# A column of norms that becomes rows through DRAM, in a two-block layer on one NeuronCore

## The chip, the cores and the metric

The kernel runs on one core of a Trainium2 chip. Its engines run side by side, each with its own queue, in order: TensorE (PE, with weight loads shown as PEld), VectorE (DVE), ScalarE (ACT), GpSimd (POOL) and SyncE (SP), which only starts DMA transfers. DMA transfers are also started from the queues of ACT and POOL. The metric is the device time of one execution in microseconds; lower is better.

## The reference

512 tokens of 1024 features pass through two blocks, in float32. The first has a mixing layer of 8 softmax-attention heads and 4 gated recurrent heads (HGRN), a cross-attention to 256 memory tokens, and a feed-forward layer. The second has a convolution branch, a state-space branch with 8 groups of 4 heads, and a gated feed-forward layer. What the change touches are two normalizations inside them. Each recurrent head of 128 features is normalized by the root of its mean square per token, before its gate:

```python
rec = hgrn2_chunkwise(gq, gf, gi, lbs[l])
rec = rmsnorm(rec, hgrn_norm_g[l]) * jax.nn.silu(gg...)   # per head of 128 features
h = h + jnp.concatenate([fox_out, rec], axis=-1) @ w_out[l]
...
def rmsnorm(x, g):
    y = x * lax.rsqrt(jnp.mean(x * x, axis=-1, keepdims=True) + EPS)
    return y * g
```

In the state-space branch each of the 8 groups of 256 features is gated and normalized in the same way, and a product with a 2048 x 1024 weight follows.

## The kernel before, in words

Tensors lie feature-major: a tile holds 128 features on the partitions and the 512 tokens along the free axis. A large product (`gemm_tile`) takes weights of 1024 x 128 at a time: SP's queue loads them, ACT casts them to a high part `wh` (L138), DVE computes the residual `wl` (L139), each into one of three buffers. For each of eight chunks PE makes three products 128x512, high by high (L150), the low part of one by the high of the other (L151, L152), which accumulate in a PSUM bank named `acc`. There are three `acc` banks, two each of `pa` and `pb`, and one `pc`. `gemm_tok` makes a token-major product and uses `pc` for its fourth tile.

A norm needs one number per token, on every partition. `col_sum` makes four products of a 128-token slice of squares with a column of ones (L223): the sums stand in a column, 128 tokens on the partitions and one column per slice. `rsqrt_col` scales them on DVE (L229) and raises them to −1/2 on POOL (L231). `row_bc` then makes four products in which the column, broadcast to 128 columns, is the stationary operand and the identity the moving one (L238); PSUM then holds the 512 values as a row on all 128 partitions. In float32 each of these is recorded as two matmuls.

Two users of this path matter here. `hgrn_out(i, AT)` writes one recurrent head, squares it, and multiplies it by the row in `pc` (L497). It is called for heads 0 and 1, and later for heads 2 and 3, in a stretch where PE also works on the attention's products and score transposes (L522), whose masks POOL adds (`fox_probs`). `group_b(g, ys, zs)` does the same for two tiles of a group (L942), and splits them into high and low parts (L201, L202). Its result is needed by `ssm_half(0)`, called in the fifth group for the first four, and `ssm_half(1)`, called after the eighth.

Next to these, `group_a` makes, per pair of heads of a group, a run of small products into `pb` (L916) whose operands come from ACT (L906) and DVE (L907), and reads rows of DRAM on all partitions by POOL's DMA (`ab`, L901; `ep`, L922). DVE also does the convolutions (L784, L807).

The order on each engine is made when the program is built: a scheduler takes the instructions in the order of the code, moved by `tc.high_priority(n)`. A negative n puts them later, so that other work already written fills in: `HPRI` is 80, `APRI` 60, `BPRI` 120. On the chip each engine keeps the order it was given.

Of the kernel before, what the change touches and what calls it, by code (L numbers as in the profile page):

```python
# [6 lines left out]
F32 = mybir.dt.float32  # L7
# [4 lines left out]
ALU = mybir.AluOpType  # L12
# [4 lines left out]
P = 128  # L17
S = 512
# [14 lines left out]
HPRI = 80  # L33
# [10 lines left out]
BPRI = 120  # L44
# [24 lines left out]
def _build(tc, nc, es, a, out):  # L69
    V, A, T, G = nc.vector, nc.scalar, nc.tensor, nc.gpsimd  # L70
# [8 lines left out]
    nrm = es.enter_context(pool("nrm", 2))  # L79
# [12 lines left out]
    def mC():  # L92
        return psc.tile([P, S], F32, tag="pc", name="pc")

    def ctile(shape, dt, name):
        return const.tile(shape, dt, tag=name, name=name)
# [3 lines left out]
    ones = ctile([P, P], F32, "ones")  # L100
    V.memset(ones, 1.0)
    es_mem, es_mx = es.enter_context(ExitStack()), ExitStack()
    mhalf = ctile([P, 4], F32, "mhalf")
    V.memset(mhalf, -0.5)

    pm = es_mem.enter_context(pool("pm", 1, side="right", reuse_waits="tile"))
# [4 lines left out]
    with tc.high_priority(3000):  # L111
        for k in range(0, 8, 2):
# [1 line left out]
            (nc.sync if k in (0, 6) else nc.gpsimd).dma_start(out=t, in_=memp[:, k:k + 2, :])  # L114
            mt += [t[:, 0, :], t[:, 1, :]]
            nc.sync.dma_start(out=raw0[:, k:k + 2, :], in_=a["w_xk"][0][:, k:k + 2, :])
    warm = nrm.tile([P, 4], F32, tag="rv", name="warm")
    A.copy(out=warm, in_=ones[:, 0:4])

    wps = psc.tile([P, S], F32, tag="pc", name="pc")  # L120
# [2 lines left out]
    ident = ctile([P, P], F32, "ident")  # L123
# [4 lines left out]
    def vcol(name, i=0, n=1):  # L128
        c, k = VEC[name]
        assert i + n <= k  # L130
        return vec[:, c + i:c + i + n]
# [76 lines left out]
    def sq_acc(accum, k, src, scale=1.0):  # L208
        if k == 0:
            A.activation(out=accum, in_=src, func=AF.Square, scale=scale)  # L210
        else:
            sq = nrm.tile([P, S], F32, tag="sq", name="sq")
            n = accum.shape[-1]
            A.activation(out=sq[:, :n], in_=src, func=AF.Square, scale=scale)
            V.tensor_tensor(out=accum, in0=accum, in1=sq[:, :n], op=ALU.add)

    def col_sum(accs, nt, ms=mA):

        ps = ms()
        accs = accs if isinstance(accs, list) else [accs]  # L220
        for j in range(nt):
            for i, ac in enumerate(accs):
                T.matmul(out=ps[:, j:j + 1], lhsT=ac[:, j * P:(j + 1) * P], rhs=ones[:, 0:1], start=i == 0,  # L223
                         stop=i == len(accs) - 1)
        return ps[:, :nt]

    def rsqrt_col(ps, nt, n, eps=EPS, name="r"):
        v = nrm.tile([P, 4], F32, tag="rv", name="rv")
        V.tensor_scalar(out=v[:, :nt], in0=ps, scalar1=1.0 / n, scalar2=eps, op0=ALU.mult, op1=ALU.add)  # L229
        r = nrm.tile([P, 4], F32, tag="rc", name="rc", bufs=4)  # L230
        G.tensor_tensor(out=r[:, :nt], in0=v[:, :nt], in1=mhalf[:, :nt], op=ALU.pow)  # L231
        return r[:, :nt]

    def row_bc(col, nt, ms=mA):

        ps = ms()
        for j in range(nt):
            T.matmul(out=ps[:, j * P:(j + 1) * P], lhsT=col[:, j:j + 1].to_broadcast([P, P]), rhs=ident, start=True,  # L238
                     stop=True)
        return ps[:, :nt * P]  # L240

    def norm(srcs, n, nt, gain=None, eps=EPS, pl=None, rtag="R", ms=mA, late=0):

# [75 lines left out]
    with ExitStack() as ea:  # L319
# [163 lines left out]
        def hgrn_out(i, AT):  # L483
            ps = mA()
            for j in range(4):
                T.matmul(out=ps[:, j * P:], lhsT=iT[:, j, i * P:(i + 1) * P],
                         rhs=AT[:, ab(j, j):ab(j, j) + 4 - j, :].rearrange("p a b -> p (a b)"),
                         start=j == 0, stop=j == 3)
            o_ = hslot(4 + i)
            mix[4 + i] = o_  # L490
            A.copy(out=o_, in_=ps)
            ac = nrm.tile([P, S], F32, tag="sqa", name="sqa")
            sq_acc(ac, 0, o_)
            with tc.high_priority(-HPRI):
                r = rsqrt_col(col_sum(ac, 4, mC), 4, P)
            with tc.high_priority(-2 * HPRI):
                V.scalar_tensor_tensor(out=o_, in0=o_, scalar=vcol("hgrn_norm_g"), in1=row_bc(r, 4, mC), op0=ALU.mult,  # L497
                                       op1=ALU.mult)

        def fox_probs(p, e, j, ps, nF, PT):  # L500

# [66 lines left out]
        hd = [hgrn_in(0), hgrn_in(1)]  # L568
        AT = hgrn_chain(hd)
        g_tok(iT, a["w_gi"])  # L570
        hgrn_out(0, AT[0])
        hgrn_out(1, AT[1])
        g_qk(0)
        g_qk(1)
        g_tok(vT, a["w_fv"])
        fox((0, 1))
        hd = [hgrn_in(2), hgrn_in(3)]
        AT = hgrn_chain(hd)
        hgrn_out(2, AT[0])
        hgrn_out(3, AT[1])  # L580
        g_qk(2)
        g_qk(3)
        fox((2, 3))
# [346 lines left out]
    def group_b(g, ys, zs):  # L930

        ac = nrm.tile([P, S], F32, tag="sqa", name="sqa")
        for e in range(2):
            V.tensor_tensor(out=zs[e], in0=ys[e], in1=zs[e], op=ALU.mult)
            sq_acc(ac, e, zs[e])
        with tc.high_priority(-APRI):
            r = rsqrt_col(col_sum(ac, 4, mC), 4, 256)
        with tc.high_priority(-BPRI):
            Rg = row_bc(r, 4, mC)
            res = []  # L940
            for e in range(2):
                V.scalar_tensor_tensor(out=zs[e], in0=zs[e], scalar=vcol("ssm_norm_g_2", 2 * g + e), in1=Rg, op0=ALU.mult,  # L942
                                       op1=ALU.mult)
                res.append(split_act(zs[e]))
        return res
# [294 lines left out]
```

## Time and profile before

| | |
|---|---|
| median of 3 runs | 1916.11 us (1915.81 to 1916.19) |
| profiled execution | 1916.54 us |
| its span | 1914.8 us |
| mean granted TensorE clock | 0.997 of full speed |
| DMA moved | 208.84 MB, mean 109 GB/s |

In the rows below, a line of a timeline has its start, its duration, the engine, the line of the program, the operation, the tiles (written <- read) with their shapes and count, and in square brackets the time the engine stood idle before it and what ended that. Matmuls are pipelined: the duration of one is longer than the distance to the next, and their ends are modelled, so distances between starts tell more than durations. A clock of 1.00 is the full level. "Waits" list who stood for whom, in total and how often.

### The profile page before, as it was taken

How to read it: one execution, taken by the hardware profiler on the slowest of the kernel's cores; microseconds unless marked ns; L12 is line 12 of the kernel's file. 1: busy time of each engine (PE TensorE's matmuls, PEld its weight loads, DVE VectorE, ACT ScalarE, POOL GpSimd, SP SyncE). 2: the span in 40 equal slices, each digit the busy share in tenths (PEclk: the TensorE clock that was granted, in tenths of full speed). 3: DMA queues.
4: the chain of work that ended last, by engine and by line, in shares of the span. 5: the costliest groups of instructions: out<-in, count | busy, mean ns of one | idle time of the engine just before them, and what ended most of it. 6: DMA issues, size and time to landing. Idle time of an engine off the chain costs nothing.

```text
span 1914.8 us, 25080 instructions
## 1 busy us (share of the span) xinstructions
PE 1892.4 (99%) x9680; PEld 1573.7 (82%) x9680; DVE 1207.1 (63%) x1886; ACT 861.7 (45%) x1393; POOL 101.8 (5%) x198
## 2 busy tenths in 40 slices
PE   9999999999999999999999999999999999999997
PEld 8887776877888888877888888888888988888897
DVE  6744756655443344467888989578997774324456
ACT  6524547444331233348545553545344653222344
POOL 1001110000000000011110110110000000000000
PEclk9999999999999999999999999999999999999999
DMA  7412212322323333344333333333345532233244
GB/s 259 132 57 86 67 54 80 100 66 78 94 95 98 99 99 104 110 95 142 119 122 108 108 119 105 107 115 103 102 141 186 165 91 98 83 116 98 90 130 145
DMA packets 67542, 208.84 MB, mean 109 GB/s; under 512 B 8536, under 2 KB 15448, under 8 KB 67424
## 3 DMA queue, kind: packets, MB, share of 16 engines
q1 hardware_dynamic: 57856, 184.09, 30.9%
q0 software_dynamic: 5968, 16.87, 3.0%
q10 hardware_dynamic: 3600, 6.30, 0.9%
q8 instruction: 76, 1.25, 0.3%
q14 instruction: 42, 0.34, 0.1%
HBM read 198.71 MB, written 8.54 MB: 108 GB/s over the span
## 4 chain that ended last, share of the span: by engine, by line
PE 51%; issue 2%; DVE 1%; DMA 1%; ACT 0%; POOL 0%; POOLq 0%; DVEq 0%; ACTq 0%
PE acc L150 16%; PE acc L151 16%; PE acc L152 16%; PE pb L916 1%; PE pa L886 1%; PE pc L238 0%; PE pa L878 0%; PE pa L868 0%; PE pc L223 0%; PE pa L238 0%; DMA ab<-acsd 0%; DMA wr<-w_dn 0%; PE pa L223 0%; POOL rc L231 0%; PE pa L861 0%
## 5 line engine op out<-in xcount | busy, mean ns | idle before, releaser
L138 ACT CAST wh<-wr 128x1024 fp32r<-128x1024 f32 (+1 forms) x343 | 347.1, 1013 | 714.7 <-PE acc L151 585.1
L139 DVE TENSOR_TENSOR wl<-wr,wh 128x1024 fp32r<-128x1024 f32 (+1 forms) x343 | 403.2, 1176 | 287.4 <-ACT wh L138 277.8
L150 PE MATMUL acc<-yh,wh 128*128 128x512 f32 (+1 forms) x1112 | 432.9, 390 | 0.1
L152 PE MATMUL acc<-yh,wl 128*128 128x512 f32 (+1 forms) x1112 | 431.2, 388 | 0.0
L151 PE MATMUL acc<-yl,wh 128*128 128x512 f32 (+1 forms) x1112 | 429.8, 387 | 0.0
L152 PE MATMUL acc<-xh,wl 128*128 128x512 f32 (+1 forms) x832 | 313.7, 377 | 0.3 <-DVE wl L139 0.3
L150 PE MATMUL acc<-xh,wh 128*128 128x512 f32 (+1 forms) x832 | 313.7, 378 | 0.3 <-DVE h L594 0.3
L151 PE MATMUL acc<-xl,wh 128*128 128x512 f32 (+1 forms) x832 | 313.1, 377 | 0.0
L150 PEld LDWEIGHTS acc<-yh,wh 128*128 128x128 f32 x1112 | 209.1, 188 | 42.0 <-issue 1.4
L152 PEld LDWEIGHTS acc<-yh,wl 128*128 128x128 f32 x1112 | 209.1, 188 | 40.9
L151 PEld LDWEIGHTS acc<-yl,wh 128*128 128x128 f32 x1112 | 209.1, 188 | 40.3 <-DVE yl L202 0.4
L150 PE MATMUL acc<-uh,wh 128*128 128x512 f32 (+1 forms) x520 | 183.9, 354 | 0.0
L151 PE MATMUL acc<-ul,wh 128*128 128x512 f32 (+1 forms) x520 | 183.7, 353 | 0.0
L152 PE MATMUL acc<-uh,wl 128*128 128x512 f32 (+1 forms) x520 | 183.6, 353 | 0.0
L807 DVE SCALAR_TENSOR_TENSOR cv<-gp,vec,cv 128x512 f32<-128x512 f32 x240 | 177.6, 748 | 6.0 <-ACT cv L805 3.0
L150 PEld LDWEIGHTS acc<-xh,wh 128*128 128x128 f32 x832 | 157.1, 189 | 29.3 <-issue 1.5
L152 PEld LDWEIGHTS acc<-xh,wl 128*128 128x128 f32 x832 | 157.2, 189 | 28.7 <-issue 1.8
L151 PEld LDWEIGHTS acc<-xl,wh 128*128 128x128 f32 x832 | 157.2, 189 | 27.0 <-issue 1.2
L152 PEld LDWEIGHTS acc<-uh,wl 128*128 128x128 f32 x520 | 98.3, 189 | 13.5
L150 PEld LDWEIGHTS acc<-uh,wh 128*128 128x128 f32 x520 | 98.3, 189 | 13.4
L151 PEld LDWEIGHTS acc<-ul,wh 128*128 128x128 f32 x520 | 98.4, 189 | 13.3
L231 POOL TENSOR_TENSOR rc<-rv,mhalf 128x4 f32<-128x4 f32 (+1 forms) x25 | 29.7, 1188 | 966.4 <-DVE rv L229 883.2
(364 smaller groups left out, 2111.8 us busy)
## 6 DMA issues: line engine op xcount, KB each, us to landing
wr<-w SPq DMA_DIRECT2D x64, 512.0 KB, 3.8
wr<-w_gu SPq DMA_DIRECT2D x44, 512.0 KB, 3.5
wr<-w_out SPq DMA_DIRECT2D x24, 512.0 KB, 3.5
wr<-w_dn SPq DMA_DIRECT2D x24, 512.0 KB, 3.6
wr<-w_xs SPq DMA_DIRECT2D x16, 512.0 KB, 3.5
wr<-w_glu SPq DMA_DIRECT2D x16, 512.0 KB, 3.5
ab<-acsd POOLq DMA_DIRECT2D x32, 256.0 KB, 3.6
wr<-w_z SPq DMA_DIRECT2D x16, 512.0 KB, 3.5
```

What stands on the lines that cost most here:

```text
L138: A.copy(out=hi[:, :n], in_=raw[:, :n])
L139: V.tensor_tensor(out=lo[:, :n], in0=raw[:, :n], in1=hi[:, :n].bitcast(F32), op=ALU.subtract)
L150: T.matmul(out=ps, lhsT=lh, rhs=rh, start=start, stop=False)
L151: T.matmul(out=ps, lhsT=lh, rhs=rl, start=False, stop=False)
L152: T.matmul(out=ps, lhsT=ll, rhs=rh, start=False, stop=stop)
L231: G.tensor_tensor(out=r[:, :nt], in0=v[:, :nt], in1=mhalf[:, :nt], op=ALU.pow)
L807: yield V.scalar_tensor_tensor(out=o, in0=gp[:, t:t + S], scalar=cw(t), in1=o, op0=ALU.mult, op1=ALU.add)
L886: T.matmul(out=ps[:, 0:256], lhsT=Bt[:, c, :], rhs=xw[:, c].rearrange("p r d -> p (r d)"), start=True, stop=True)
L916: m = T.matmul(out=dst[r * 64:r * 64 + 64, c * P:(c + 1) * P], lhsT=lh, rhs=rh, start=True, stop=True)
```

## The change

A new function `row_far` takes the place of `row_bc` for all four recurrent heads and for the groups 0 to 6 (group 7 keeps `row_bc`). It transposes the column by one product: nt columns of 128 become nt rows of 128 in PSUM. ACT copies them to SBUF, a DMA from ACT's queue writes them to DRAM, and a DMA from POOL's queue reads them back on all 128 partitions, 512 tokens long (256 KB), into a tile of the pool's "sqa" tag. DVE multiplies by that tile instead of by PSUM, at a later place (−2·BPRI for the groups, −3·HPRI for the heads). For the heads, a new `hgrn_norm` joins two: eight column sums, one power of 128x8, one transpose of eight columns, one write, and two reads. The tiles for the column grow from 4 to 8 columns. The diff, without a third widened tile (a dummy at the start):

```diff
@@ -100,7 +100,7 @@
     ones = ctile([P, P], F32, "ones")
     V.memset(ones, 1.0)
     es_mem, es_mx = es.enter_context(ExitStack()), ExitStack()
-    mhalf = ctile([P, 4], F32, "mhalf")
+    mhalf = ctile([P, 8], F32, "mhalf")
     V.memset(mhalf, -0.5)
 
     pm = es_mem.enter_context(pool("pm", 1, side="right", reuse_waits="tile"))
@@ -225,9 +225,9 @@
         return ps[:, :nt]
 
     def rsqrt_col(ps, nt, n, eps=EPS, name="r"):
-        v = nrm.tile([P, 4], F32, tag="rv", name="rv")
+        v = nrm.tile([P, 8], F32, tag="rv", name="rv")
         V.tensor_scalar(out=v[:, :nt], in0=ps, scalar1=1.0 / n, scalar2=eps, op0=ALU.mult, op1=ALU.add)
-        r = nrm.tile([P, 4], F32, tag="rc", name="rc", bufs=4)
+        r = nrm.tile([P, 8], F32, tag="rc", name="rc", bufs=4)
         G.tensor_tensor(out=r[:, :nt], in0=v[:, :nt], in1=mhalf[:, :nt], op=ALU.pow)
         return r[:, :nt]
 
@@ -238,6 +238,18 @@
             T.matmul(out=ps[:, j * P:(j + 1) * P], lhsT=col[:, j:j + 1].to_broadcast([P, P]), rhs=ident, start=True,
                      stop=True)
         return ps[:, :nt * P]
+
+    def row_far(col, nt, dst, ms=mA):
+
+        ps = ms()
+        T.transpose(out=ps[0:nt, 0:P], in_=col, identity=ident)
+        t = nrm.tile([8, P], F32, tag="sq", name="rt")
+        A.copy(out=t[0:nt], in_=ps[0:nt, 0:P])
+        d = dram.tile([8, P], F32, tag="rd", name="rd", bufs=4)
+        nc.scalar.dma_start(out=d[0:nt], in_=t[0:nt])
+        for i, x in enumerate(dst):
+            G.dma_start(out=x, in_=d[4 * i:4 * i + 4].rearrange("a b -> (a b)").unsqueeze(0).partition_broadcast(P))
+        return dst
 
     def norm(srcs, n, nt, gain=None, eps=EPS, pl=None, rtag="R", ms=mA, late=0):
 
@@ -491,11 +503,20 @@
             A.copy(out=o_, in_=ps)
             ac = nrm.tile([P, S], F32, tag="sqa", name="sqa")
             sq_acc(ac, 0, o_)
+            return ac
+
+        def hgrn_norm(i, acs):
+
             with tc.high_priority(-HPRI):
-                r = rsqrt_col(col_sum(ac, 4, mC), 4, P)
+                ps = mC()
+                for ac, c in zip(acs, (0, 4)):
+                    col_sum(ac, 4, lambda: ps[:, c:c + 4])
+                r = rsqrt_col(ps[:, 0:8], 8, P)
             with tc.high_priority(-2 * HPRI):
-                V.scalar_tensor_tensor(out=o_, in0=o_, scalar=vcol("hgrn_norm_g"), in1=row_bc(r, 4, mC), op0=ALU.mult,
-                                       op1=ALU.mult)
+                Rs = row_far(r, 8, [nrm.tile([P, S], F32, tag="sqa", name="Rh") for _ in range(2)], mC)
+            with tc.high_priority(-3 * HPRI):
+                for o_, R in zip(mix[4 + i:6 + i], Rs):
+                    V.scalar_tensor_tensor(out=o_, in0=o_, scalar=vcol("hgrn_norm_g"), in1=R, op0=ALU.mult, op1=ALU.mult)
 
         def fox_probs(p, e, j, ps, nF, PT):
 
@@ -568,16 +589,14 @@
         hd = [hgrn_in(0), hgrn_in(1)]
         AT = hgrn_chain(hd)
         g_tok(iT, a["w_gi"])
-        hgrn_out(0, AT[0])
-        hgrn_out(1, AT[1])
+        hgrn_norm(0, [hgrn_out(i, AT[i]) for i in range(2)])
         g_qk(0)
         g_qk(1)
         g_tok(vT, a["w_fv"])
         fox((0, 1))
         hd = [hgrn_in(2), hgrn_in(3)]
         AT = hgrn_chain(hd)
-        hgrn_out(2, AT[0])
-        hgrn_out(3, AT[1])
+        hgrn_norm(2, [hgrn_out(2 + i, AT[i]) for i in range(2)])
         g_qk(2)
         g_qk(3)
         fox((2, 3))
@@ -935,9 +954,13 @@
             sq_acc(ac, e, zs[e])
         with tc.high_priority(-APRI):
             r = rsqrt_col(col_sum(ac, 4, mC), 4, 256)
+        res = []
         with tc.high_priority(-BPRI):
-            Rg = row_bc(r, 4, mC)
-            res = []
+            if g < 7:
+                Rg = row_far(r, 4, [nrm.tile([P, S], F32, tag="sqa", name="Rg")], mC)[0]
+            else:
+                Rg = row_bc(r, 4, mC)
+        with tc.high_priority(-2 * BPRI if g < 7 else -BPRI):
             for e in range(2):
                 V.scalar_tensor_tensor(out=zs[e], in0=zs[e], scalar=vcol("ssm_norm_g_2", 2 * g + e), in1=Rg, op0=ALU.mult,
                                        op1=ALU.mult)
```

Three places of the new order follow. The first is PE in the first group; in the trace of before, its first row starts at 933.67 us. `yh` and `yl` are the high and low parts of the block's input, `rc` the column, `mt`, `xd`, `Ct` and `st` operands of `group_a`. Before:

```order
L150 MATMUL acc<-yh,wh 128x512
L238 MATMUL pc<-ident,rc 128x128
L151 MATMUL acc<-yl,wh 128x512
L238 MATMUL pc<-ident,rc 128x128
L152 MATMUL acc<-yh,wl 128x512
L916 MATMUL pb<-mt,xd 64x128 x8
L916 MATMUL pb<-Ct,st 64x128 x6
L238 MATMUL pc<-ident,rc 128x128 x2
L150 MATMUL acc<-yh,wh 128x512
L151 MATMUL acc<-yl,wh 128x512
```

And PE at the same place of the order after, where L916 has become L935:

```order
L150 MATMUL acc<-yh,wh 128x512
L245 MATMUL pc<-ident,rc 4x128
L151 MATMUL acc<-yl,wh 128x512
L152 MATMUL acc<-yh,wl 128x512
L150 MATMUL acc<-yh,wh 128x512
L151 MATMUL acc<-yl,wh 128x512
L935 MATMUL pb<-mt,xd 64x128 x8
L935 MATMUL pb<-Ct,st 64x128 x6
L152 MATMUL acc<-yh,wl 128x512
```

One product stands where four stood, and the run of small products begins two large products later.

The second is PE at the recurrent heads 0 and 1, before (`sqa` holds the squares, `Sx` the attention's scores, the last row is the fourth tile of `gemm_tok`):

```order
L151 MATMUL acc<-wl,xh 128x512
L238 MATMUL pc<-ident,rc 128x128
L152 MATMUL acc<-wh,xl 128x512
L238 MATMUL pc<-ident,rc 128x128
L150 MATMUL acc<-wh,xh 128x512
L151 MATMUL acc<-wl,xh 128x512
L152 MATMUL acc<-wh,xl 128x512
L150 MATMUL acc<-wh,xh 128x512
L151 MATMUL acc<-wl,xh 128x512
L223 MATMUL pc<-ones,sqa 128x1 x4
L152 MATMUL acc<-wh,xl 128x512
L150 MATMUL acc<-wh,xh 128x512
```

After those rows come four L238 in one piece, two products into `acc`, two L522, and the first product into `pc`. The same stretch of PE after:

```order
L150 MATMUL acc<-wh,xh 128x512
L151 MATMUL acc<-wl,xh 128x512
L152 MATMUL acc<-wh,xl 128x512
L245 MATMUL pc<-ident,rc 8x128
L150 MATMUL acc<-wh,xh 128x512
L151 MATMUL acc<-wl,xh 128x512
L150 MATMUL pc<-wh,xh 128x512
L151 MATMUL pc<-wl,xh 128x512
```

The column sums of both heads now stand together, 61 large products ahead of L245, and two large products lie between L245 and the next user of `pc`. At heads 2 and 3, twelve large products lie between the last sum and L245.

The third is DVE in the second group (`zs` are the two tiles to be normalized, `Rg` the rows read back, `cv` and `xt` are convolutions, `y` and `ep` belong to `group_a`). Before:

```order
L139 TENSOR_TENSOR wl<-wr,wh 128x1024
L924 SCALAR_TENSOR_TENSOR y<-xt,vec,pb 128x512
L925 TENSOR_TENSOR ep<-pb,ep 128x384
L942 SCALAR_TENSOR_TENSOR zs<-zs,vec,pc 128x512
L926 TENSOR_TENSOR y<-y,ep 128x384
```

After, from the same weight residual on:

```order
L139 TENSOR_TENSOR wl<-wr,wh 128x1024
L943 SCALAR_TENSOR_TENSOR y<-xt,vec,pb 128x512
L803 SCALAR_TENSOR_TENSOR xt<-xp,vec,xt 128x512
L944 TENSOR_TENSOR ep<-pb,ep 128x384
L803 SCALAR_TENSOR_TENSOR xt<-xp,vec,xt 128x512
L945 TENSOR_TENSOR y<-y,ep 128x384
L826 SCALAR_TENSOR_TENSOR cv_7779<-gp,vec,cv_7779 128x512
L803 SCALAR_TENSOR_TENSOR xt<-xp,vec,xt 128x512
L826 SCALAR_TENSOR_TENSOR cv_7779<-gp,vec,cv_7779 128x512
L965 SCALAR_TENSOR_TENSOR zs<-zs,vec,Rg 128x512
```

The multiply stood third behind the residual and stands ninth. A second one follows two rows later, and then the next residual. On ACT the row's write stands directly behind the weight cast of this stretch; on POOL the read-back stands between two issues of `ab`, and at the heads between mask additions of the attention.

## Rows read from the trace of the kernel before

**Rows 1.** The page, busy microseconds of each engine, share and instructions
```profile
PE 1892.4 (99%) x9680; PEld 1573.7 (82%) x9680; DVE 1207.1 (63%) x1886; ACT 861.7 (45%) x1393; POOL 101.8 (5%) x198
```
**Rows 2.** Windows: length, PE, PEld, DVE, ACT, POOL, PEclk, DMA share, GB/s
```profile
1000.00:1020.00 20.00, 20.00 (x95) 16.52 (x92) 18.89 (x28) 16.49 (x33) 2.34 (x6) 1.00 0.41 127
```
**Rows 3.** Waits: who waited for whom, us in total, times, longest
```profile
ACT wh L138 <- PE acc L151: 585.1, 231, 5.4
```
**Rows 4.** Timeline of PE in the groups, 930 to 938.5 us
```profile
930.17 0.40 PE L152 MATMUL acc<-yh,wl 128*128 128x512 f32 x1
...
932.51 0.39 PE L151 MATMUL acc<-yl,wh 128*128 128x512 f32 x1
...
933.67 0.40 PE L150 MATMUL acc<-yh,wh 128*128 128x512 f32 x1
...
937.38 0.39 PE L151 MATMUL acc<-yl,wh 128*128 128x512 f32 x1
...
938.29 0.40 PE L152 MATMUL acc<-yh,wl 128*128 128x512 f32 x1
```
**Rows 5.** Timeline of PE at heads 0 and 1, 161 to 169 us
```profile
161.66 0.39 PE L152 MATMUL acc<-wh,xl 128*128 128x512 f32 x1
...
164.64 0.95 PE L223 MATMUL pc<-ones,sqa 128*128 128x1 f32 x8
...
166.94 1.16 PE L238 MATMUL pc<-ident,rc 128*128 128x128 f32 x8 [0.78 <-POOL rc L231]
...
168.17 0.40 PE L152 MATMUL acc<-wh,xl 128*128 128x512 f32 x1
```
**Rows 6.** Timeline of PE at heads 2 and 3, 263 to 272 us
```profile
263.61 0.39 PE L152 MATMUL acc<-xh,wl 128*128 128x512 f32 x1
...
264.96 0.39 PE L151 MATMUL acc<-xl,wh 128*128 128x512 f32 x1
...
268.05 0.40 PE L150 MATMUL acc<-xh,wh 128*128 128x512 f32 x1
269.29 1.16 PE L238 MATMUL pc<-ident,rc 128*128 128x128 f32 x8 [0.84 <-POOL rc L231]
...
270.52 0.39 PE L152 MATMUL acc<-xh,wl 128*128 128x512 f32 x1
270.75 0.27 PE L522 MATMUL pb<-ident,Sx 128*128 128x128 f32 x1
...
271.09 0.39 PE L151 MATMUL acc<-xl,wh 128*128 128x512 f32 x1
```
**Rows 7.** Timeline of PE, transposes on part of the array, 79.5 to 84 us
```profile
80.08 0.39 PE L152 MATMUL acc<-xh,wl 128*128 128x512 f32 x1
80.40 0.22 PE L347 MATMUL pc<-ident,Fr 8*128 8x8 f32 x1
...
82.65 0.40 PE L151 MATMUL acc<-xl,wh 128*128 128x512 f32 x1
```
**Rows 8.** Groups of lines by form, PEld: count | busy, mean ns | idle before
```profile
L916 PEld LDWEIGHTS pb<-mt,xd 128*64 128x64 f32 x256 | 13.6, 136 | 4.9 <-DVE st L893 2.6 <-issue 1.8 <-DVE mt L907 0.4
...
L522 PEld LDWEIGHTS pb<-ident,Sx 128*128 128x128 f32 x80 | 9.7, 142 | 7.2 <-issue 4.3 <-PE pb L522 0.6 <-PE acc L151 0.4
```
**Rows 9.** Timelines of ACT, DVE and PE in the second group, 996 to 1018.5 us
```profile
998.21 1.05 ACT L138 CAST wh<-wr 128x1024 fp32r<-128x1024 f32 x1 [1.77 <-PE acc L151]
...
1008.44 1.23 DVE L139 TENSOR_TENSOR wl<-wr,wh 128x1024 fp32r<-128x1024 f32 x1 [1.11 <-ACT wh L138]
...
1017.60 0.39 PE L152 MATMUL acc<-yh,wl 128*128 128x512 f32 x1
```
**Rows 10.** DMA issues: queue, count, KB each, median us to landing
```profile
gated<-gt ACTq DMA_DIRECT2D x16, 256.0 KB, 2.0
...
ab<-acsd POOLq DMA_DIRECT2D x32, 256.0 KB, 3.6
...
eacd<-s__6619 POOLq DMA_DIRECT2D x1, 64.0 KB, 9.0
```

More of the change, by code (lines that the diff above doesn't have):

```diff
@@ L116, in _build @@
             nc.sync.dma_start(out=raw0[:, k:k + 2, :], in_=a["w_xk"][0][:, k:k + 2, :])
-    warm = nrm.tile([P, 4], F32, tag="rv", name="warm")
+    warm = nrm.tile([P, 8], F32, tag="rv", name="warm")[:, 0:4]
     A.copy(out=warm, in_=ones[:, 0:4])
```

## The prediction

> **What bounds the kernel now.** I read the busy totals first, then the windows of the groups' stretch, then the waits, and last TensorE's timeline at each place where the change takes something out. The totals show TensorE (PE) busy for 99% of the span, VectorE (DVE) for 63%, ScalarE (ACT) for 45% and GpSimd (POOL) for 5% [rows 1]. In 20 us of the groups' stretch PE works all 20.00 us at granted clock 1.00, so there a microsecond of PE work is a microsecond of span; DVE is at 18.89 us in the same window, close behind [rows 2]. The waits say which way the others look: ACT's weight cast stands 585.1 us in all for a product that frees a buffer [rows 3]. Weights are early, PE is late. So the forecast is a sum over PE's order, provided that nothing new makes PE wait.
>
> The unit is the accumulating 128x512 product: four starts lie between 937.38 and 938.29, 0.2275 us each [rows 4]. What another piece costs is the distance between two such products around it, less 0.2275 for every product in it.
>
> **What goes.** In the groups: between the start at 933.67 and that at 937.38 lie four of those products, the 28-record L916 block, and the four broadcast products of L238 for one group. 3.71 − 4 × 0.2275 = 2.80. The same block without L238 lies between 930.17 and 932.51, with two products: 2.34 − 0.455 = 1.885. The difference, 0.91 us, is what the four L238 products cost, 0.23 each [rows 4]. Seven groups make 6.4; I take 0.90 each, 6.3.
>
> Heads 0 and 1: 161.66 to 168.17 holds twelve accumulating products (2.73), the column sums of one head (0.95, they stay) and both heads' L238. 6.51 − 2.73 − 0.95 = 2.83 us, in which 0.78 of waiting for POOL's power is included [rows 5]. Heads 2 and 3: 263.61 to 264.96 with two products is 1.35 − 0.455 = 0.90; 268.05 to 270.52, two products, is 2.47 − 0.455 = 2.02, with 0.84 of the same wait [rows 6]. Together 2.91. These waits go too, since the row's step stands 61 accumulating products after the last sum for the first pair and 12 (2.7 us) for the second; before, the second head's L238 stood one or two behind. What is late next is the same PE, so a stall removed is time won. Sum removed: 6.3 + 2.8 + 2.9 = 12.0 us.
>
> **What comes on PE.** Nine transposes of the column (L245), two of 8 columns and seven of 4, each with 128 columns moving. No row shows a stationary operand of 4 columns. Bound from below: one full-width transpose L522 between two products, 270.52 to 271.09, is 0.57 − 0.455 = 0.115 us [rows 6], and nothing suggests less, since the same 128 columns move. From above: four L347 transposes, which use 8 rows of the array and move 8 columns, stretch 80.08 to 82.65 with five products: 2.57 − 1.14 = 1.43, or 0.36 each [rows 7]; with 128 instead of 8 moving columns, half of a two-record L238 product (0.23 / 2 = 0.11) more, 0.47. I take 0.36, the row of the nearest kind, a lone product on part of the array between full ones: 9 × 0.36 = 3.2, ends 1.0 and 4.2.
>
> The loads of such operands are where a rule of the skill leans the other way. The row first: a 64-column operand loads in 136 ns and a 128-column one in 142 [rows 8], so half the columns save 6 ns. The Trainium skill, "TensorE: Matmul & The Clock Gate", section "LDWEIGHTS (loading the stationary operand)", has a load time proportional to the columns, which would make one of 4 columns nearly free. The rows do not bear that out between 64 and 128; by the rule the nine steps would cost the lower end or less, and the sum would come to about −11 instead of −8.3.
>
> **What comes beside PE.** Per step: an ACT copy of at most 8 x 128, a DMA issue on ACT's queue, one or two on POOL's, and a DVE multiply that reads SBUF where it read PSUM. POOL is at 5%, ACT has 3.5 us free of 20 even in the fullest window [rows 1, 2]. I cost them at nothing; what hides them is PE's backlog.
>
> The round trip stands in front of DVE's multiply, and DVE runs in order: weight residuals wait behind it. For the second group: the row's DMA stands behind ACT's cast that ends at 998.21 + 1.05 = 999.3 [rows 9]. A write from ACT's queue lands in 2.0 us, POOL's issue takes about 0.6, a broadcast read of the same 256 KB lands in 3.6 [rows 10]: 1005.5. In the new order the multiply is ninth behind a weight residual that begins as that cast ends; 1.23 for the residual [rows 9] plus eight times the window's mean of 18.89 / 28 = 0.67 [rows 2] is 1005.9. About level. The next residual begins at 1008.44, after 1.11 us of standing idle, ends at 1009.67, and PE reads it first at 1017.60 [rows 9]: 7.9 us in hand. The multiply's own result is needed far later: `ssm_half(0)` is called in the fifth group, `ssm_half(1)` after the eighth. I cost it at nothing on PE.
>
> **What waits newly.** In the first pair only two accumulating products (0.455 us) stand between L245 and the next product into pc, a bank with one buffer; that product must wait until ACT has copied the row out. With a copy of some 0.5 us (half of the 1.05 us in which ACT casts 1024 columns [rows 9]) and a hand-over, I take 0.3 us. If the copy stands behind such a cast, it is some 1.1 more, 1.5 at the upper end; if ACT is quick, nothing. In the second pair the power is 8 columns wide and may still run after 2.7 us; bounded by nothing and by the 0.84 of the old wait [rows 6], I take 0.2. POOL's reads stand among fox's mask additions: pair one's two issues wait there for the landing of the write, and mask additions, and DVE's scores, queue behind.
>
> **Sum.** −12.0 + 3.2 + 0.5 = −8.3 us. The profiled execution took 1916.54 us (span 1914.8), 0.43 above the median of the timed runs, 1916.11. From the former 1908.2, from the latter 1907.8. I forecast 1907.8.
>
> **Rivals.**
> *Cheap transposes.* The narrow step costs what a full-width one does, 0.115, and nothing waits: −12.0 + 1.0 = −11.0, 1905.1. For it: the same moving columns, PE's backlog. Against: the 0.36 of L347.
>
> *The heads' gain comes back as waits.* The pc bank in pair one at 1.5 us, and POOL's stop in front of fox's mask additions in each pair for a write's landing of 2.0 us less what DVE has in hand: with about 3 us together the pairs' net gain of 2.8 + 2.9 − 0.7 = 5.0 shrinks to 0.5, and the groups' 6.3 − 2.5 = 3.8 remains: −4.3, and with a slow narrow product (0.47) −3.3: 1912.5. For it: pairs' old waits show PE close to its suppliers there. Against: they were waits for one POOL operation that leaves the path.
>
> *Late rows (slower).* DVE stands in order at the groups' multiply until the read lands; residuals fall behind; PE runs out of weights. It decides once the trip of 6.2 us has grown by 0.4 + 7.9 = 8.3, to 14.5 us; from there each microsecond costs one in each of seven groups, and at 15.7 us the gain of 8.3 is gone. If write and read both took the 9.0 us of the slowest issue from POOL's queue [rows 10], the trip would be 18.6 and the loss 7 × 4.1 = 29: 1936.5. For it: DVE at 94% of the window catches up slowly. Against: the same kind of read lands in 3.6.
>
> *That the change removes less than it says* I give nothing: the new order lacks 44 L238 products and has 9 of L245.
>
> **Chances and range.** Forecast 0.65, its own range 1905.4 to 1910.5 (narrow product 0.115 to 0.47, waits 0 to 1.5). Cheap transposes 0.14. Heads' gain lost 0.12. Late rows 0.09. The measurement can tell 0.2%, 3.8 us, from no change. Faster by more takes the forecast and the cheap transposes, 0.79, and a little of the third: 0.80; within 0.2%: 0.12; slower: 0.08. The range runs from 1904.5 to 1912.6; outside lie the late rows and some of both flanks, 0.18.
>
> **What would show it.** In the profile after: no L238 in groups 0 to 6 and both pairs; the distance between accumulating products around a group's L245 about 0.36 over pitch (0.1 if the rival holds); no idle of PE at L245 for POOL's power, 0.3 of idle before the first L150 into pc in pair one; ACT's weight cast still waiting for PE for over 550 us; DVE's wait for Rg under 3 us per group; PE idle in the groups near nothing. The forecast is wrong if PE shows waits for wl or wh in the groups, if DVE's standing for Rg or Rh exceeds 8 us, or if the half-clock level appears in a stretch that ran at 1.00.

## The result and the profile after

The changed kernel took 1904.88 us (median of 4 runs, 1904.75 to 1905.93) against 1916.15 for the kernel before beside it: ratio 0.9941, 95% interval 0.9924 to 0.9958. That is 11.3 us faster where 8.3 were forecast: inside the stated range (1904.5 to 1912.6), but beyond the forecast's own (1905.4 to 1910.5), and where the rival of the cheap transposes had it (1905.1). A later pair of runs gave 1905.55 against 1916.35, 0.9939 (0.9927 to 0.9952).

Its profiled execution took 1905.93 us with a span of 1904.2. The page's first part answers to [rows 1]:

```profile
PE 1882.7 (99%) x9601; PEld 1563.1 (82%) x9601; DVE 1206.9 (63%) x1884; ACT 861.9 (45%) x1402; POOL 107.2 (6%) x207
```

PE is busy 9.7 us less and still for 99%; DVE, ACT and POOL did not lighten. So the kernel is shorter because PE has less to do, and it is bound as before. A window of 20 us in the second group (columns as in [rows 2]) and the weight casts' wait, which answers to [rows 3]:

```profile
992.00:1012.00 20.00, 20.00 (x110) 16.64 (x108) 19.69 (x28) 17.38 (x35) 3.05 (x8) 1.00 0.47 151
```
```profile
ACT wh L138 <- PE acc L151: 592.9, 230, 5.7
```

PE has no idle there, and ACT waits for PE longer than before (592.9 for 585.1 us). DVE is busier (19.69 for 18.89), but the two windows do not hold quite the same work: over some 480 us of the groups it is busy 406 us in place of 403.

All traces hold the same 8016 accumulating products (L150 to L152), in the changed kernel all but 16 of them at the same place of PE's order as before, so the start of the k-th in one can be compared with that in the other. How far a kernel leads before (negative is earlier), by how much that changed in each stretch, in us of before's timeline:

```
stretch of before    129 to 354   354 to 911   911 to 1384   1384 to 1459
                     heads        neither      groups        end of groups
changed kernel         -5.83        -0.14        -5.34          +0.61
changed, again         -6.01        -2.61        -5.36          +0.63
heads only             -5.90        -2.64        +0.01          -0.02
groups only            -0.04        -2.08        -5.36          +0.68
multiply later         -6.60        -2.40        -5.35          +0.68
column by DMA          +3.24        -2.78       +20.39          +9.50
group 7 too            -5.75        -2.28        -5.35          +4.01
more rows              -6.60        +1.55        -5.34          +0.69
one-pass sums          -7.72        -1.28        -8.94          +1.05
all that paid          -8.28        -0.78        -8.94          +0.78
```

The second column, where only "more rows" and "all that paid" change anything, scatters by 2.6 us among the others: a spell at the half clock (below), which the traces of before and of the first changed run have and most others do not, and, at 880 us, a wait of 0.2 to 1.5 us for ACT. The other columns repeat within 0.3.

PE around the first group's new transpose, which answers to [rows 4]:

```profile
927.58 0.39 PE L150 MATMUL acc<-yh,wh 128*128 128x512 f32 x1
927.81 0.27 PE L245 MATMUL pc<-ident,rc 128*4 128x128 f32 x1
927.83 0.47 PE L151 MATMUL acc<-yl,wh 128*128 128x512 f32 x1
928.14 0.39 PE L152 MATMUL acc<-yh,wl 128*128 128x512 f32 x1
```

927.58 to 928.14 holds two products: 0.56 − 0.455 = 0.105 us for the transpose (0.11 by the starts before rounding). All nine lie between 0.11 and 0.12. For heads 0 and 1, in place of [rows 5]:

```profile
163.82 0.39 PE L152 MATMUL acc<-wh,xl 128*128 128x512 f32 x1
164.05 0.27 PE L245 MATMUL pc<-ident,rc 128*8 128x128 f32 x1
...
164.39 0.40 PE L151 MATMUL acc<-wl,xh 128*128 128x512 f32 x1
164.66 0.50 PE L150 MATMUL pc<-wh,xh 128*128 128x512 f32 x1
```

No wait for POOL is left, and the first product into pc starts 0.27 us after its neighbour: ACT's copy out of the single bank cost 0.04 beyond a pitch. For heads 2 and 3 ([rows 6]) the 0.84 us for POOL is gone as well, but a new wait stands behind it, on DVE first and then on PE:

```profile
268.22 0.75 DVE L519 SCALAR_TENSOR_TENSOR mix<-mix,vec,Rh 128x512 f32<-128x512 f32 x1 [1.84 <-DMA Rh<-rd]
269.28 0.75 DVE L519 SCALAR_TENSOR_TENSOR mix<-mix,vec,Rh 128x512 f32<-128x512 f32 x1 [0.31 <-DMA Rh<-rd]
...
273.85 0.41 PE L543 MATMUL pb<-ident,Sx 128*128 128x128 f32 x2 [1.00 <-DVE Sx L534]
```

DVE stands in order for the rows read back while the attention's scores queue behind it, and PE then waits 1.00 us for them. In the groups the trip runs like this (second group, timelines of ACT's queue, POOL and DVE):

```profile
991.28 0.27 ACTq L249 DMA_DIRECT2D rd<-rt  x1
...
993.24 0.54 POOL L251 DMA_DIRECT2D Rg<-rd  x1 [1.08 <-DMA rd<-rt]
...
998.35 0.75 DVE L965 SCALAR_TENSOR_TENSOR zs<-zs,vec,Rg 128x512 f32<-128x512 f32 x1
```

Issue to issue 1.96 us, then 4.7 us (median of the seven reads) to landing, 6.7 in all, where 6.2 was estimated; DVE reaches the multiply at 998.35 without standing. Not in every group: in the fifth, DVE stands for the rows,

```profile
1226.89 1.42 DVE L965 SCALAR_TENSOR_TENSOR zs<-zs,vec,Rg 128x512 f32<-128x512 f32 x2 [3.09 <-DMA Rg<-rd]
```

for 3.1 us here and 3.9 in the profile of the later pair. PE has no idle time there, and the group's gain is 0.72 where the other six gave 0.76 to 0.79. Last, at the end of the groups DVE is late once: PE waits 0.32 us at 1429.57 for a sum (L983) that frees a bank, and with the slower products around it this is the +0.6 of the last column.

### The profile page after: what moved, and what is told of

It reads as the page before. It is cut to its first block, busy times and chain, and to the rows that moved or that the text cites. A ratio compares the mean times of both kernels' runs of the same rounds, so it can differ in the third digit from the quotient of the medians.

```text
span 1904.2 us, 24959 instructions
## 1 busy us (share of the span) xinstructions
PE 1882.7 (99%) x9601; PEld 1563.1 (82%) x9601; DVE 1206.9 (63%) x1884; ACT 861.9 (45%) x1402; POOL 107.2 (6%) x207
## 3 DMA queue, kind: packets, MB, share of 16 engines
q10 hardware_dynamic: 3688, 6.32, 1.0%
## 4 chain that ended last, share of the span: by engine, by line
PE 51%; issue 2%; DVE 1%; ACT 0%; DMA 0%; POOL 0%; POOLq 0%; DVEq 0%; ACTq 0%
PE acc L150 16%; PE acc L152 16%; PE acc L151 16%; PE pb L935 1%; PE pa L905 1%; PE pa L897 0%; PE pa L887 0%; PE pc L223 0%; DMA ab<-acsd 0%; PE pa L238 0%; PE pa L223 0%; POOL rc L231 0%; DVE yl L202 0%; PE pa L880 0%; DVE f L1175 0%
## 5 line engine op out<-in xcount | busy, mean ns | idle before, releaser
L138 ACT CAST wh<-wr 128x1024 fp32r<-128x1024 f32 (+1 forms) x343 | 347.2, 1013 | 720.8 <-PE acc L151 592.9
L150 PE MATMUL acc<-yh,wh 128*128 128x512 f32 (+1 forms) x1112 | 432.4, 389 | 0.4 <-DVE so L983 0.3
L152 PE MATMUL acc<-yh,wl 128*128 128x512 f32 (+1 forms) x1112 | 431.5, 388 | 0.0
L152 PE MATMUL acc<-xh,wl 128*128 128x512 f32 (+1 forms) x832 | 314.4, 378 | 0.3 <-DVE wl L139 0.3
L150 PE MATMUL acc<-xh,wh 128*128 128x512 f32 (+1 forms) x832 | 313.1, 377 | 0.3 <-DVE h L613 0.3
L150 PEld LDWEIGHTS acc<-yh,wh 128*128 128x128 f32 x1112 | 209.1, 188 | 42.5 <-issue 1.4
L152 PEld LDWEIGHTS acc<-yh,wl 128*128 128x128 f32 x1112 | 209.0, 188 | 42.0 <-issue 1.2
L150 PE MATMUL acc<-uh,wh 128*128 128x512 f32 (+1 forms) x520 | 183.9, 354 | 0.0
L152 PE MATMUL acc<-uh,wl 128*128 128x512 f32 (+1 forms) x520 | 183.7, 353 | 0.0
L152 PEld LDWEIGHTS acc<-xh,wl 128*128 128x128 f32 x832 | 157.3, 189 | 28.9 <-issue 2.4
L150 PEld LDWEIGHTS acc<-xh,wh 128*128 128x128 f32 x832 | 157.1, 189 | 28.6 <-ACT xh L201 0.9
L150 PEld LDWEIGHTS acc<-uh,wh 128*128 128x128 f32 x520 | 98.3, 189 | 13.6
L152 PEld LDWEIGHTS acc<-uh,wl 128*128 128x128 f32 x520 | 98.3, 189 | 13.4
L231 POOL TENSOR_TENSOR rc<-rv,mhalf 128x4 f32<-128x4 f32 (+2 forms) x23 | 27.1, 1178 | 961.5 <-DVE rv L229 876.1
```

The source lines that it names most:

```text
L138: A.copy(out=hi[:, :n], in_=raw[:, :n])
L150: T.matmul(out=ps, lhsT=lh, rhs=rh, start=start, stop=False)
L152: T.matmul(out=ps, lhsT=ll, rhs=rh, start=False, stop=stop)
```

## The experiments

The theory: the time is PE's order. A removed broadcast gives its 0.23 us, a transpose costs 0.11, and nothing else counts but waits that PE shows. The rivals are those of the prediction and others named in the expectations.

**The two halves.** Heads as changed, groups as before (`if g < 7` became `if g < 0`, and the multiply's priority −BPRI):

> The four recurrent heads as in the changed kernel, all eight groups as before. Theory 'PE's order is the time' (each removed broadcast product gives its 0.23 us, each transpose takes 0.115, and waits count only where PE shows them): in a product-by-product comparison with before the lead over before grows to about 6.0 us by the end of the attention and then stays level through the groups; time about 1910.2 us, 6 below before. Rival 'indirect': part of the heads' gain comes from other work that the new order displaces, and is given back later, so the lead shrinks after 300 us, to 3 to 4 us.

And groups as changed, each head again on its own with `row_bc`:

> Groups 0 to 6 as in the changed kernel, the recurrent heads as before. Theory 'PE's order is the time': nothing until 900 us, then seven steps of 0.77 to 0.79 us (0.91 less 0.115), 5.4 in all; time about 1910.8 us, and the two halves add up to the whole change, 11.3. Rival 'indirect': steps of another size than 0.8, or a sum of both halves that differs from 11.3 by over 1 us.

Measured: 1910.10 us against 1916.68, ratio 0.9967 (0.9954 to 0.998), and 1910.88, ratio 0.9967 (0.9955 to 0.9979). The table has the halves as −5.90 with nothing in the groups, and −5.36 with nothing in the heads; the second half also carries the +0.68. The lead of the heads stays after the attention. The sum, 6.58 + 5.80 = 12.4 by medians, lies 1.1 above 11.3, just beyond the 1 us that the rival names, but it is not sharp to 1 us; by the trace −5.90 − 5.36 + 0.68 = −10.58 is what the whole change has in these stretches (−10.56). "Indirect" falls, but for the 0.6 at the end.

**What a transpose costs.** More products by the identity, each alone between large ones (but for that of 128 columns, which the scheduler put directly behind the first), and L347 on more rows of the array. The diff in parts:

```diff
+        if twice:
+            if twice == 2:
+                T.matmul(out=ps[0:nt, P:2 * P], lhsT=col, rhs=ident, start=True, stop=True)
+            elif twice == 4:
+                T.transpose(out=ps[0:nt, P:2 * P], in_=col, identity=ident)
+            else:
+                T.transpose(out=ps[0:twice, P:2 * P], in_=tri[:, 0:twice], identity=ident)
...
-                    T.transpose(out=ps[:, j * 8:(j + 1) * 8], in_=Fr[:, j * P:(j + 1) * P], identity=ident[0:8, 0:8])
...
+                    R_ = (8, 32, 64, 128)[j]
+                    T.transpose(out=ps[:, j * 128:j * 128 + R_], in_=FR[0:R_, j * P:(j + 1) * P], identity=ident[0:R_, 0:R_])
```

> The changed kernel with a second product by the identity placed alone between accumulating products in groups 1 to 6: transposes of 8, 32, 64 and 128 columns, a second one of 4, and one float32 matmul (two records) of 4 columns. And the four transposes L347 of the attention's sums with 8, 32, 64 and 128 rows of the array instead of 8 each. If the 128 moving columns set the price: 0.11 to 0.12 us at each width, 0.23 for the float32 matmul. If a narrow stationary operand saves its load: cheaper at 4 columns than at 128 by up to 0.1. If work on part of the array costs extra, as the prediction took it: 0.36 at 4 to 64 columns and 0.115 at 128. For L347: 0.36 at 8 rows and falling to about 0.12 at 128 rows if the rows are the cause; the same 0.36 at all if they are not. Time about 1 us above the changed kernel.

1906.24 us (one run). Against the changed kernel, product by product, the second one costs 0.12 us at 8 columns, 0.13 at 32, 0.11 at 64, 0.12 at 128 and 0.11 at 4. PE at the 8-column one:

```profile
989.82 0.40 PE L150 MATMUL acc<-yh,wh 128*128 128x512 f32 x1
990.06 0.27 PE L245 MATMUL pc<-ident,rc 128*4 128x128 f32 x1
...
990.40 0.27 PE L252 MATMUL pc<-ident,tri 128*8 128x128 f32 x1
...
990.75 0.40 PE L150 MATMUL acc<-yh,wh 128*128 128x512 f32 x1
```

Three products lie from 989.82 to 990.75: 0.93 − 0.68 = 0.25 for two transposes. The width does not matter to a transpose. For the float32 matmul of 4 columns:

```profile
1332.06 0.40 PE L150 MATMUL acc<-yh,wh 128*128 128x512 f32 x1
...
1332.73 0.38 PE L248 MATMUL pc<-ident,rc 128*4 128x128 f32 x2
...
1333.38 0.40 PE L150 MATMUL acc<-yh,wh 128*128 128x512 f32 x1
```

1.32 − 0.68 − 0.12 = 0.52 us, over twice the 0.23 of L238 with 128 columns, and not the 0.23 expected; where its loads stand is shown at the end, why they stand there is not. And the L347 transposes (L369 here), 8, 32, 64 and 128 rows in turn:

```profile
81.08 0.22 PE L369 MATMUL pc<-ident,Fr 8*128 8x8 f32 x1
...
81.67 0.24 PE L369 MATMUL pc<-ident,Fr 32*128 32x32 f32 x1
...
82.27 0.27 PE L369 MATMUL pc<-ident,Fr 64*128 64x64 f32 x1
...
82.82 0.27 PE L369 MATMUL pc<-ident,Fr 128*128 128x128 f32 x1
```

From start to start 0.59, 0.60 and 0.55 with one large product between, so 0.36, 0.37 and 0.32 for 8, 32 and 64 rows. With all four on 128 rows ("more rows", below) they cost 1.00 us less together than the 1.43 of [rows 7], 0.11 each. Rows of the array left out are what costs a transpose; columns left out cost it nothing, though they do cost the float32 matmul above.

**The stall at heads 2 and 3.** Their multiply joined with the gate, behind the scores:

```diff
...
+            if R is not None:
+                V.scalar_tensor_tensor(out=t, in0=t, scalar=vcol("hgrn_norm_g"), in1=R, op0=ALU.mult, op1=ALU.mult)
             V.tensor_tensor(out=mix[4 + i], in0=mix[4 + i], in1=t, op=ALU.mult)
...
```

> The changed kernel, but heads 2 and 3 are multiplied by their rows only together with their gates, after the attention's scores. Theory 'DVE in order': the 1.00 us for which PE waits for the scores at 273.9 us comes from DVE standing 1.84 and 0.31 us for the rows in front of them; with the multiply moved away DVE scores at once, PE's wait goes, and the kernel gains 1.0 us against the changed one, about 1903.9 us. Rival: the scores are late for another reason (POOL's mask additions behind the row's read, ACT's table loads), PE's wait of about 1 us stays, and the time is that of the changed kernel, 1904.9.

1905.63 us, 0.9943 (0.9926 to 0.9959): no difference from the changed kernel that runs can tell. The trace can: PE's waits for scores, of the changed kernel and of this one,

```profile
PE pb L543 <- DVE Sx L534: 1.0, 1, 1.0
PE pb L543 <- DVE Sx L540: 0.6, 2, 0.3
```
```profile
PE pb L547 <- DVE Sx L544: 0.6, 2, 0.4
```

The wait of 1.0 is gone, and the heads' lead is 6.60 in place of 5.83. DVE in order was the cause; 0.77 of the 1.00 stayed won.

**A long trip.** No transpose; the column goes to DRAM as single values:

```diff
-        ps = ms()
-        T.transpose(out=ps[0:nt, 0:P], in_=col, identity=ident)
-        t = nrm.tile([8, P], F32, tag="sq", name="rt")
-        A.copy(out=t[0:nt], in_=ps[0:nt, 0:P])
         d = dram.tile([8, P], F32, tag="rd", name="rd", bufs=4)
-        nc.scalar.dma_start(out=d[0:nt], in_=t[0:nt])
+        nc.scalar.dma_start(out=d[0:nt].rearrange("a b -> b a"), in_=col)
```

> The changed kernel without the transpose, ACT's copy and the pc bank: ACT's queue writes the column itself to DRAM, as 512 (heads: 1024) single values at a stride, and POOL's queue reads rows back as before. It asks whether a long round trip costs PE anything. In the order the groups' multiply stands some 16 places earlier on DVE than in the changed kernel. Theory 'covered': PE loses 9 x 0.115 = 1.0 us of work more, a scattered write may take longer than the 2.0 us of a plain one, DVE stands for it, and as long as it stands less than the 7 us by which weights are early, PE waits for nothing: about 1903.9 us. Rival 'late rows': DVE stands over 8 us per group, weight residuals come late, PE waits for wl in the groups, and the kernel is several us slower than the changed one.

1948.32 us (one run). "Late rows" holds. The trip in the second group:

```profile
998.78 0.38 ACTq L245 DMA_DIRECT2D rd<-rc  x1
...
1007.04 0.60 POOL L247 DMA_DIRECT2D Rg<-rd  x1 [8.29 <-DMA rd<-rc]
...
1012.24 0.75 DVE L961 SCALAR_TENSOR_TENSOR zs<-zs,vec,Rg 128x512 f32<-128x512 f32 x1 [8.88 <-DMA Rg<-rd]
```

The write takes 8.3 us where the row's took 2.0, the trip 13.5, and DVE stands 8.88. The multiply also stands earlier in DVE's order, ahead of the weight residual that it follows in the changed kernel, so DVE reaches it 4.6 us behind the write's issue where it took 7.1. The Trainium skill, "DMA: Bandwidth & Descriptors", section "Rules for kernel authors", says that an access whose last dimension is strided becomes one descriptor per element; this run agrees: the packets of ACT's queue grow from 3688 to 9376 for the same 6.32 MB, by about the 5632 values written, and the same 512 values take four times as long. Some of the waits, and PE at heads 2 and 3:

```profile
PE pc L223 <- DVE sqa L215: 7.7, 3, 4.7
PE acc L150 <- ACT xh L201: 6.9, 1, 6.9
PE acc L152 <- DVE wl L139: 3.1, 7, 0.8
```
```profile
275.42 0.47 PE L539 MATMUL pb<-ident,Sx 128*128 128x128 f32 x1 [7.58 <-DVE Sx L536]
```
```profile
DVE Sx L530 <- POOL nD L525: 16.6, 2, 9.0
```
```profile
1300.00:1362.00 62.00, 56.71 (x270) 46.24 (x269) 48.52 (x71) 29.77 (x52) 6.55 (x12) 0.94 0.37 108
```

PE waits more for squares and casts than for weight residuals. At the heads POOL stands in front of the mask additions, DVE's scores wait for these, and PE for the scores, as the rival of the heads had it: the two pairs lie 9.1 us behind the changed kernel (3.24 + 5.83). Late in the groups stretches with idle time of PE also show a lower granted clock (0.94 on average). Whether DVE standing or POOL standing before its `ab` reads weighs more in the groups was not separated.

**The last group too** (`if g < 8`):

> The changed kernel with the last group's rows through DRAM as well. Here nothing lies far behind: in PE's order 39 products (8.9 us) stand between the transpose and the first product that reads the normalized group. From rows of the changed kernel the way is: copy 0.3, write 2.0, issue 0.5, read 4.7, multiply 0.75, cast 0.6, about 9 us with nothing queued ahead of it. Theory: the product is 0.8 us cheaper as in the other groups, but PE waits 0 to 3 us for the cast, so the kernel is between 0.8 us faster and 2 us slower than the changed one, and PE's waits show ACT's xh for the first time. Rival 'a trip is always hidden': 0.8 us faster, no wait. Rival 'a trip is exposed in full': over 5 us slower.

1909.0 us (one run). The group gives 0.7 to 0.8, and PE never waits for its cast: the scheduler put other products ahead. The loss comes 30 us later, in the norm of the convolution, whose sums and broadcast now stand with nothing between them:

```profile
1409.80 1.02 PE L223 MATMUL pa<-ones,sqa 128*128 128x1 f32 x8 [1.04 <-DVE sqa L215]
1412.27 1.30 PE L238 MATMUL pa<-ident,rc 128*128 128x128 f32 x8 [1.45 <-POOL rc L231]
```
```profile
1412.00:1416.00 4.00, 3.73 (x15) 3.15 (x16) 2.66 (x5) 1.57 (x3) 0.21 (x1) 0.64 0.56 187
```

Both waits are followed by 4 us at a clock of 0.64. By the trace the kernel lies 3.3 us behind the changed one, outside the range expected, and for another reason than expected.

**More rows through DRAM**, with the later multiply and the padded L347 (`row_far(r, nt, [R], ms)` in `norm_fin` for two norms, `row_far(r1, 4, [R1])`):

> The changed kernel with the later multiply of heads 2 and 3, the four transposes L347 padded to 128 rows of the array, and three more broadcasts replaced by a row through DRAM: the norms before the cross-attention and before the feed-forward layer, and the stored row of the output norm. Theory 'price list' against the changed kernel: multiply 0.8, the padded transposes 4 x 0.24 = 0.95, the cross-attention norm 0.9 + 0.8 of wait for POOL - 0.115 = 1.6, the feed-forward norm 0.8, the stored row 0.8 to 1.4: 5 to 5.5 us, about 1899.7 us. Rival: the trip is exposed at the norms (their rows are needed to empty the accumulating banks), PE waits several us there, and the kernel gains 2 us or less, or loses.

1906.3 us, 0.9953 (0.9936 to 0.997): no gain, the rival. The padding gave 1.00, all of it at that place. The cross-attention's norm gave 0.3 of the 1.6 expected: between 354 and 413 us the lead grows by 1.75, and by 1.41 in the kernel with the later multiply alone, both at full clock; POOL's 0.8 us stay in front of the transpose, and PE waits 0.94 us for a weight cast a little later. The feed-forward norm lost it all:

```profile
487.55 0.47 PE L150 MATMUL acc<-xh,wh 128*128 128x512 f32 x1 [1.91 <-DVE t L709]
```
```profile
488.00:492.00 4.00, 4.00 (x13) 3.10 (x12) 3.35 (x6) 3.10 (x6) 0.00 (x0) 0.57 0.43 135
```

PE waits 1.91 us for the exposed row and then runs 4 us at 0.57, with products 0.43 apart instead of 0.23: the lead falls by 3.1 there. The stored row gave nothing that lasted.

**The sums that remain.** The squares rounded to the large products' type, one pass (`ac` as F32R, −0.5 for the ones):

```diff
+            T.matmul(out=ps[:, 2 * j:2 * j + 2], lhsT=ac[:, j * P:(j + 1) * P], rhs=mh_r[:, 0:2], start=True, stop=True)
```

> The changed kernel with the squares of the groups and of the recurrent heads rounded to the type of the large products, so that each of their 48 column-sum products is one pass instead of two (the squares are rounded, the sum is not otherwise changed). Theory 'records': a two-pass product with one moving column costs 0.225 and one pass half of it, 0.11, so each norm gives 0.45 us, 12 of them 5.4 us: about 1899.5 us. Rival: the one-pass product costs as much because loading 128 columns of weights sets the price, or DVE's additional work in the groups takes it back: within 1 us of the changed kernel.

1900.56 us, 0.9919 (0.9904 to 0.9934); the trace has −7.72 and −8.94, 5.5 beyond the changed kernel, of which 0.4 is given back at the end of the groups.

```profile
148.03 0.48 PE L152 MATMUL acc<-xl,wh 128*128 128x512 f32 x1
148.34 0.17 PE L221 MATMUL pc<-mhalf,sqa 128*128 128x2 f32 x1
148.37 0.48 PE L153 MATMUL acc<-xh,wl 128*128 128x512 f32 x1
```

0.34 − 0.2275 = 0.11 for each, as expected. Halving the records halves passes and loads alike (96 of each become 48), so this run does not tell which of them sets the price; that a load does not is what the ladder shows, where 4 to 128 columns cost the same.

**All that paid together:**

> What paid so far, together: the changed kernel with one-pass column sums in the groups and recurrent heads, the later multiply of heads 2 and 3, the four transposes L347 on all 128 rows of the array, and the row of the norm before the cross-attention through DRAM (not that of the feed-forward norm, where PE waited 1.9 us and then ran at the half clock, nor that of the last group). Against the changed kernel, run beside it: 4.4 (sums) + 0.8 (multiply) + 1.0 (transposes) + 1.6 (norm) = 7.8 us, about 1897 us. Rival: the pieces share the same DVE and give back a part, as in the kernel with more rows: 4 to 5 us.

1896.34 us, 0.9894 (0.9879 to 0.9909), 20.0 below before. The changed kernel beside it:

> The changed kernel unaltered, for its distance from before on the same chip and as the neighbour of the other kernel of this call: 11 us below before, 10.5 to 11.5.

1905.55, 10.8 below before. So 9.2 us come on top of the change. The trace can place some 7 of them: against the changed kernel 2.3 to 2.5 at the heads and 3.6 in the groups (table), 1.0 in the padded transposes ahead of them, and 0.1 to 0.3 at the norm. The other 2 us are not placed; single runs of the changed kernel lie between 1902.97 and 1905.93.

## Why the prediction was right, and where it was off

- *Bound by PE's order, everything else hidden in the groups.* Right. The casts' wait stayed above 550 us, PE shows no wait for weights in the groups, and each group gave 0.72 to 0.79.
- *12.0 us removed.* Right within what the halves can tell: 7 × 0.77 with 0.11 per transpose put back is 0.88 per group (0.90 taken), and the heads' 5.83 with 0.23 for two transposes and the new wait of 1.00 added is 7.1 against 5.74. Some 1.2 of the surplus of 1.3 lies between 183 and 219 us, where the scores' small products stand in fewer, longer runs between large ones and a wait of 0.30 for DVE is gone. The prediction had no term for it.
- *Nine transposes at 0.36.* This is the step that failed, a mis-sized term: 0.11 each, 1.0 in place of 3.2, the lower bound and the "cheap transposes" rival's number. L347, taken as the nearest row because it too uses part of the array, leaves out rows, the new step leaves out columns. The ladder shows that only the first costs a transpose. The Trainium skill, "TensorEngine Tiling (Array Packing)", section "Key Properties", says that a change of tiling mode drains the engine: the transposes on 8 to 64 rows agree with it (0.32 to 0.37 against 0.11), those of few columns, which the profile writes 128*4, don't (0.11 to 0.12), and the float32 matmul of 4 columns (0.52 against 0.23) would again.
- *0.3 at pc and 0.2 for the power.* 0.04 and nothing. The wait came elsewhere: 1.00 at heads 2 and 3, from DVE standing for the rows. That is the mechanism of the late rows, in another place, at a third of the 3 us that the heads' rival charged for POOL's stop.
- *Late rows.* Not in the changed kernel, but shown to be real by the long trip. Its point of decision, 14.5 us of trip, is not tested by that run's 13.5, since DVE reaches the multiply 2.5 us sooner there. By the standing: 3.1 and 3.9 us of it cost PE nothing in the fifth group of the changed kernel, as the 7.9 us in hand had it. The long trip's 8.8 to 9.8 us are 0.9 to 1.9 beyond that cover and cost 3.7 us per group against the changed kernel ((20.39 + 5.34) / 7, with the lower clock in it), two to four times what one for one would give. The cover was read from one residual that DVE makes early; squares and casts stand in the same queue, and PE waited more for them.
- *No cost at the end.* DVE's order gave 0.6 back there.

Errors of 2.2 (transposes), 0.5 (waits) and 1.3 (surplus) toward faster, against 1.0 (the new wait) and 0.6 (the end) toward slower, leave 2.4 us: 8.3 becomes 10.7, where 10.8 and 11.3 were measured. That the time is that of the cheap transposes' rival is in part luck: it had neither the surplus of 1.3 nor the 1.6 lost at heads 2 and 3 and at the end, and these nearly cancel.

Three sums of the prediction are off by little. The heads' rival with a slow narrow product comes to 1912.8, not 1912.5. The upper end of the forecast's own range adds up to 1910.0 (−12.0 + 4.2 + 1.5 + 0.2), not 1910.5. The column sums at heads 0 and 1 cost 0.90 by the distance of the products around them; 0.95 is their duration.

## What to carry to other kernels

Where one engine has no idle time, price a change from the distance between its big instructions around each small one, and take the price of a new form from a row with the same part of the array in use, not from one that merely looks as small. Work handed to DMA is free only as long as the in-order engine that waits for it has nothing urgent queued behind. Look for the slot before moving more: the same edit gave 0.8 us in each group and cost 3 us at a norm without cover.

## What the runs showed of the hardware

The weight load of an identity product takes 83 ns at 4 columns, 95 at 32, 110 at 64 and 139 at 128 (columns: count | busy us, mean ns | idle before):

```profile
L245 PEld LDWEIGHTS pc<-ident,rc 128*4 128x4 f32 x7 | 0.6, 83 | 0.3
...
L252 PEld LDWEIGHTS pc<-ident,tri 128*128 128x128 f32 x1 | 0.1, 139 | 0.1
...
L252 PEld LDWEIGHTS pc<-ident,tri 128*64 128x64 f32 x1 | 0.1, 110 | 0.0
L252 PEld LDWEIGHTS pc<-ident,tri 128*32 128x32 f32 x1 | 0.1, 95 | 0.0
```

The Trainium skill's rule that load time goes with the columns ("TensorE: Matmul & The Clock Gate", section "LDWEIGHTS (loading the stationary operand)") holds here for the direction and not for the proportion: 4 and 8 columns take the same 82 to 84 ns. The prediction read 6 ns for half the columns from loads in runs of small products (136 and 142); alone between large ones the half saves 29. None of it reached the distance between products.

What goes with the price is when a load begins. On 8 rows it begins when its product does (81.08), on 128 rows 0.22 us ahead (82.60 for 82.82), and for the float32 matmul of 4 columns with its product again (1332.73):

```profile
81.08 0.13 PEld L369 LDWEIGHTS pc<-ident,Fr 8*128 8x128 f32 x1 [0.35 <-issue]
...
82.60 0.14 PEld L369 LDWEIGHTS pc<-ident,Fr 128*128 128x128 f32 x1
```
```profile
1332.73 0.09 PEld L248 LDWEIGHTS pc<-ident,rc 128*4 128x4 f32 x2 [0.24 <-issue]
```

The products that cost more are those whose load did not go ahead. What kept it back is not shown.

The clock did not answer in the same way to the same idle time. Windows of the changed kernel and of the heads-only kernel at the norm before the cross-attention, where PE waits 0.31 and then 0.8 us:

```profile
359.00:363.00 4.00, 2.90 (x17) 2.44 (x17) 0.44 (x2) 1.04 (x1) 1.03 (x1) 0.84 0.18 74
363.00:367.00 4.00, 4.00 (x16) 3.37 (x16) 2.56 (x4) 1.37 (x3) 0.00 (x0) 0.73 0.08 11
```
```profile
359.00:363.00 4.00, 2.89 (x17) 1.96 (x16) 1.34 (x3) 1.36 (x2) 1.03 (x1) 1.00 0.36 131
363.00:367.00 4.00, 4.00 (x23) 3.24 (x23) 2.67 (x4) 1.53 (x4) 0.00 (x0) 1.00 0.10 12
```

PE is busy 2.90 and 2.89 of the first 4 us. One kernel gets 0.84 there and 0.73 in the next window, a mix of the two levels 1.2 and 2.4 GHz, the other the full level throughout. It cost 1.4 us here, of the 2.5 us by which the two profiled executions of the changed kernel differ in the second column of the table. What it costs in the timed runs is not shown, since one run of each was profiled.
